# Attention in a two-layer decoder: row maximum from the high parts alone, full scores with keys on partitions, row sums on GpSimd

## The chip, the cores and the metric

One core of a Trainium2 chip. The time is the device time of one execution in microseconds (us). The core's engines are TensorE (PE in the profile; PEld its weight loads), VectorE (DVE), ScalarE (ACT), GpSimd (POOL) and SyncE (SP, which here only issues transfers). Each engine takes its own instructions in order and waits for the others by semaphores.

## What is computed

A Mamba-2 layer, then a latent-attention layer with 16 heads over 2048 tokens, in float32. The change touches only the attention, which per head h computes:

```python
s = (q_nope . k_nope + q_rope . k_rope) * 96 ** -0.5      # 64 + 32 features
p = softmax(where(key <= query, s, -inf))
o = p @ v                                                 # 64 features
```

A softmax row needs its maximum m, the exponentials exp(s - m), and their sum; o is divided by the sum at the end. Queries and keys are kept as a pair of parts, high and low, whose sum is the float32 number; three products (high by high, high by low, low by high) make one full score.

## The kernel before

`layers` runs the Mamba layer and the projections of the second layer, which write queries, keys, values and gates to DRAM. `attention` calls `heads`; `back` applies gate, reciprocal sums and the output projection. A scheduler sets the order of the instructions on DVE, ACT, POOL and SP; in `heads` the order on PE is as written.

A job is a head and a block of 512 queries (64 jobs). In a job the keys up to the diagonal are taken, 1 to 4 blocks of 512.

- `scores`: for each of the four groups of 128 queries, and each piece of up to 512 keys, three products (L86 to L88, in `mm3`) with **queries on the partitions**; Q is the weight, K moves. The last piece gets the causal mask as a product with the identity (L1014, L1016). DVE reduces each piece to its maximum (L1017); when all pieces of the group are there, to the negated row maximum nm (L1021). ACT then takes the exponential out of PSUM, with nm as its bias and the row sum as a second result (L1029), into the float32 tile Pr; DVE adds the sums of the pieces (L1033).
- `turn`: the value product needs keys on the partitions, so each 128 x 128 block of Pr is transposed on PE (L1044), four into a bank. `pair16` makes two float16 parts of it: ACT copies the high part (L117), DVE subtracts it from the PSUM bank for the low part (L118).
- `values`: two products with V as the weight (L1054, L1055), summed over the keys in one bank O. `finish` copies O to Os (ACT, L1061) and writes it out in two halves: SP stores the first (L1063), POOL issues an adding transfer of the second to the same place (L1067), which waits until the first has landed. After a head's last job the reciprocal sums are transposed (L1073) and stored.

The four groups' scores run 20 steps ahead (`LAG`); the table `CREDIT` says which transposes (T) and value products (V) follow each step. `load_k`, `load_v` and `load_q` fetch the next head's tiles on POOL's queue (L944 to L958). All PSUM tiles are banks of one pool, `pp`, with the tags mm and tr, four banks each. For `back` ACT and POOL split the output weights (L1127, L1128) during the last heads.

Of the kernel before, what the change touches and what calls it, by code (L numbers as in the profile page):

```python
# [21 lines left out]
P = 128  # L22
# [15 lines left out]
NP = 24  # L38
# [3 lines left out]
LAG = 20  # L42
DEPTH = 2
CREDIT = (
    (("VT",), ("TV",), ("VT",), ("TV",)),
    (("", "VTVT"), ("", "TTVV"), ("", "TTVV"), ("", "TTVV")),
    (("TT", "", "VVTV"), ("TV", "", "VTTV"), ("TV", "", "TTVV"), ("TTV", "", "TVV")),
    (("T", "", "", "VVTTVTV"), ("T", "V", "", "VTTVTV"), ("T", "V", "V", "TVTTV"), ("TV", "V", "", "TVTVT")),
)
MAGIC = 12582912.0  # L50
PSCALE = 32768.0
# [18 lines left out]
class Net:  # L70
# [180 lines left out]
    def constants(self, cp):  # L251
# [4 lines left out]
        self.mk = cp.tile([P, 2 * P], BF16, name="mk")  # L256
        at = 0
# [4 lines left out]
    def layer_constants(self, cp):  # L262
# [13 lines left out]
        nc.vector.memset(self.mk[:, P:], NEG)  # L276
        self.wdt = cp.tile([P, KD, 2, H], F16, name="wdt")
# [19 lines left out]
        nc.vector.tensor_copy(self.mk[:, 0:P], self.mask)  # L297

# [73 lines left out]
    def value_scale(self):  # L372
# [4 lines left out]
        for n in range(2):  # L377
# [18 lines left out]
            v.tensor_scalar(e, e, -25, None, ALU.add)  # L396
# [526 lines left out]
    def open_heads(self):  # L923
# [5 lines left out]
        self.load_k(0, 0, NB - 1)  # L929

    def load_vq(self):

        self.load_k(0, NB - 1, NB)
        self.load_q(0, 0)
        self.load_v(0)
        for n in range(1, NB):
            self.load_q(0, n)

    def load_k(self, h, lo, hi):

        nc, ts = self.nc, slice(lo * TB, hi * TB)
        if lo == 0:
            self.keys[h] = self.t(self.hp, "K", [96, 2, T], F32R, bufs=2)
        nc.gpsimd.dma_start(self.keys[h][0:64, :, ts], self.kn_d[h * 64:(h + 1) * 64, :, ts])  # L944
        nc.gpsimd.dma_start(self.keys[h][64:96, :, ts], self.kr_d[:, :, ts])

    def load_v(self, h):

        V = self.vals[h] = self.t(self.xq, "xT", [P, T // P, P], F16, bufs=8)
        self.nc.gpsimd.dma_start(V, self.v_d[:, h * P:(h + 1) * P].rearrange("(k p) d -> p k d", p=P))  # L950

    def load_q(self, h, n):

        nc, ts = self.nc, slice(n * TB, (n + 1) * TB)
        Q = self.quer[h, n] = self.t(self.xq, "xT", [96, 2, TB], F32R, bufs=8)
        nc.gpsimd.dma_start(Q[0:64], self.qn_d[h * 64:(h + 1) * 64, :, ts])
        nc.gpsimd.dma_start(Q[64:80], self.q1_d[h * 16:(h + 1) * 16, :, ts])
        nc.gpsimd.dma_start(Q[80:96], self.q2_d[h * 16:(h + 1) * 16, :, ts])  # L958

# [343 lines left out]
```

## Time and profile before

| | |
|---|---|
| median of 3 runs | 3202.09 us (3199.31 to 3207.09) |
| profiled execution | 3204.34 us, span 3202.6 us from first to last instruction |
| mean granted TensorE clock | 0.995 |
| busy share of the span | PE 96%, DVE 75%, ACT 60%, POOL 19% |
| first score product to last value product of the attention | 2087.6 to 3011.8 us |
| one head | 57.17 us |

The row of an instruction group reads: line, engine, operation, out<-in by the kernel's names, shape, count | busy us, mean ns of one | idle time of the engine just ahead of it, and what ended it. A row of one tile or line reads: least / median / most ns. A row of the timeline reads: start, duration, engine, line. Instructions of PE and ACT overlap their neighbours, so the distance between two starts is the price of one more, and the duration is its latency.

### The profile page before, as it was taken

How to read it: one execution, taken by the hardware profiler on the slowest of the kernel's cores; microseconds unless marked ns; L12 is line 12 of the kernel's file. 1: busy time of each engine (PE TensorE's matmuls, PEld its weight loads, DVE VectorE, ACT ScalarE, POOL GpSimd, SP SyncE). 2: the span in 40 equal slices, each digit the busy share in tenths (PEclk: the TensorE clock that was granted, in tenths of full speed). 3: DMA queues.
4: the chain of work that ended last, by engine and by line, in shares of the span. 5: the costliest groups of instructions: out<-in, count | busy, mean ns of one | idle time of the engine just before them, and what ended most of it. 6: DMA issues, size and time to landing. Idle time of an engine off the chain costs nothing.

```text
span 3202.6 us, 51345 instructions
## 1 busy us (share of the span) xinstructions
PE 3085.4 (96%) x17744; PEld 2163.4 (68%) x17744; DVE 2401.2 (75%) x5178; ACT 1914.1 (60%) x4817; POOL 609.1 (19%) x842
## 2 busy tenths in 40 slices
PE   6999999999999999999999999999999999999998
PEld 3455555666655566665878888877777777777777
DVE  7778887767677676767876665678888888888675
ACT  8667554444455444455645554477877778778522
POOL 0212122121122212212111211322212122222100
PEclk9999999999999999999999999999999999999999
DMA  8667645334443345334476656853444434443485
GB/s 285 229 214 230 229 144 194 127 126 145 141 157 130 115 151 189 127 128 142 141 271 218 225 190 194 265 111 78 95 81 84 81 78 96 79 97 99 101 270 159
DMA packets 207113, 497.61 MB, mean 155 GB/s; under 512 B 27746, under 2 KB 51042, under 8 KB 205412
## 3 DMA queue, kind: packets, MB, share of 16 engines
q1 hardware_dynamic: 165444, 370.04, 35.6%
q0 software_dynamic: 41408, 124.29, 15.9%
q8 instruction: 140, 2.29, 0.3%
q14 instruction: 121, 0.99, 0.1%
HBM read 362.22 MB, written 131.99 MB: 154 GB/s over the span
## 4 chain that ended last, share of the span: by engine, by line
PE 64%; DVE 13%; ACT 8%; DMA 8%; issue 6%; POOL 1%; SPq 0%; ACTq 0%; DVEq 0%; POOLq 0%
PE mm L86 13%; PE mm L87 12%; PE mm L88 12%; PE tr L1044 6%; PE tr L87 3%; PE tr L1054 3%; PE tr L1055 3%; PE tr L86 3%; PE tr L88 3%; DVE cacc L460 3%; DMA big<-cumT 2%; DMA wraw<-in_ssm_w_in_dram 1%; DVE big L634 1%; ACT Pr L1029 1%; PE tr L656 1%
## 5 line engine op out<-in xcount | busy, mean ns | idle before, releaser
L118 DVE SCALAR_TENSOR_TENSOR PTs<-tr,PTs 128x512 f16<-128x512 f32 (+3 forms) x640 | 374.9, 607 | 93.9 <-ACT PTs L117 86.8
L117 ACT ACTIVATE PTs<-tr 128x512 f16<-128x512 f32 (+3 forms) x640 | 328.5, 541 | 141.4 <-PE tr L1044 140.3
L1017 DVE TENSOR_REDUCE mx<-mm 128x1 f32<-128x512 f32 (+2 forms) x631 | 375.7, 608 | 45.7 <-PE mm L88 42.6
L1029 ACT ACTIVATE Pr<-mm,nm 128x512 f32<-128x512 f32 (+2 forms) x631 | 395.7, 636 | 23.1 <-DVE nm L1021 21.4
L1044 PE MATMUL tr<-pack,Pr 128*128 128x128 f32 x2176 | 317.6, 273 | 1.0 <-ACT Os L1061 0.9
L86 PE MATMUL mm<-K,xT 96*128 96x512 f32 (+2 forms) x639 | 288.2, 451 | 23.3 <-ACT Pr L1029 21.8
L86 PE MATMUL mm<-xT,wsp 128*128 128x512 f16 (+1 forms) x800 | 304.9, 381 | 0.3 <-DVE sz L484 0.3
L88 PE MATMUL mm<-xT,wsp 128*128 128x512 f16 (+1 forms) x800 | 303.4, 380 | 1.4 <-DVE wsp L118 1.3
L87 PE MATMUL mm<-xT,wsp 128*128 128x512 f16 (+1 forms) x800 | 303.7, 380 | 0.0
L1044 PEld LDWEIGHTS tr<-pack,Pr 128*128 128x128 f32 x2176 | 253.5, 141 | 49.7 <-ACT Os L1061 1.7
L648 ACT ACTIVATE Xw<-tr,d_wend 128x64 f32<-128x64 f32 x512 | 183.4, 359 | 133.3 <-DVE Xd L644 133.3
L460 DVE SCALAR_TENSOR_TENSOR cacc<-craw,pack,cacc 128x512 f32<-128x512 f32 x288 | 213.6, 764 | 30.5 <-ACT cacc L458 28.9
L86 PE MATMUL mm<-wsp,xT 128*128 128x512 f16 (+1 forms) x640 | 232.4, 363 | 1.6 <-ACT craw L454 1.6
L88 PE MATMUL mm<-K,xT 96*128 96x512 f32 (+2 forms) x639 | 231.6, 362 | 0.0
L87 PE MATMUL mm<-wsp,xT 128*128 128x512 f16 (+1 forms) x640 | 231.6, 362 | 0.0
L87 PE MATMUL mm<-K,xT 96*128 96x512 f32 (+2 forms) x639 | 231.4, 362 | 0.0
L88 PE MATMUL mm<-wsp,xT 128*128 128x512 f16 (+1 forms) x640 | 231.1, 362 | 0.0
L1054 PE MATMUL tr<-PTs,xT 128*128 128x512 f16 (+3 forms) x640 | 222.0, 348 | 0.1
L86 PE MATMUL mm<-wsp,yT 128*128 128x512 f32 x512 | 208.1, 409 | 13.3 <-DVE sz L484 4.7
L1055 PE MATMUL tr<-PTs,xT 128*128 128x512 f16 (+3 forms) x640 | 219.4, 347 | 0.0
L606 POOL TENSOR_TENSOR Xp<-Xw,Xp 128x512 fp32r<-128x512 f32 x64 | 81.8, 1278 | 711.3 <-ACT Xp L605 382.4
L88 PE MATMUL mm<-wsp,yT 128*128 128x512 f32 x512 | 203.0, 397 | 1.4 <-DVE yT L110 1.4
(411 smaller groups left out, 7418.2 us busy)
## 6 DMA issues: line engine op xcount, KB each, us to landing
wsp<-wi_d SPq DMA_DIRECT2D x96, 512.0 KB, 3.7
wsp<-wo_d SPq DMA_DIRECT2D x96, 512.0 KB, 3.5
big<-cumT SPq DMA_DIRECT2D x64, 512.0 KB, 4.9
wi_d<-wsp SPq DMA_DIRECT2D x32, 512.0 KB, 3.4
wo_d<-wsp SPq DMA_DIRECT2D x64, 256.0 KB, 2.5
xT<-qn_d POOLq DMA_DIRECT2D x64, 256.0 KB, 4.4
K<-kn_d POOLq DMA_DIRECT2D x15, 1024.0 KB, 9.2
hx<-in_ssm_w_in_dram SPq DMA_DIRECT2D x48, 256.0 KB, 4.3
```

Of the source, the lines that this page charges most:

```text
L86: mm(out, l_hi, r_hi, start=start, stop=False)
L87: mm(out, l_hi, r_lo, start=False, stop=False)
L88: mm(out, l_lo, r_hi, start=False, stop=stop)
L117: self.nc.scalar.activation(hi, src, AF.Copy, scale=scale)
L118: self.nc.vector.scalar_tensor_tensor(lo, src, scale, hi, ALU.mult, ALU.subtract)
L460: nc.vector.scalar_tensor_tensor(acc, raw[:, k:k + TB], wk[k], acc, ALU.mult, ALU.add)
L648: act(Xw[:, hc], px[:, hc], AF.Copy, scale=wend[:, h0 + h:h0 + h + 1])
L1017: v.tensor_reduce(mx[:, n:n + 1], s[:, :w], AX.X, ALU.max)
L1029: nc.scalar.activation(x[:, :w], s[:, :w], AF.Exp, bias=nm, accum_out=sm[:, n:n + 1])
L1044: nc.tensor.transpose(pt[:, j * P:(j + 1) * P], st["P"][j][kb], self.ident)
L1054: nc.tensor.matmul(st["O"][:, c], vals[h][:, kb, :], u[:, 0], start=kb == 0, stop=False)
L1055: nc.tensor.matmul(st["O"][:, c], vals[h][:, kb, :], u[:, 1], start=False, stop=kb == nk - 1)
```

## The change

**Maximum pass (`tops`).** For each group of 128 queries one product, high part by high part, goes over all keys, with the mask as before, into M: two banks, one buffer. DVE reduces both banks in one instruction (L1019, or L1021 for one bank): one step for up to two pieces. After a job's last step POOL negates the maximum, adds the constant `LIFT` (ln 64), splits the result into high and low parts (L1029 to L1031), and SP stores them to DRAM and reads them back as **row 96 of the query tile** (L1033, L1034). The key tile has a row 96 too: ones in the high part, zeros in the low, written to DRAM once when the kernel starts.

**Full scores (`probs`).** K is the weight, 128 keys; Q moves, 512 queries, 97 rows. So the three products give s - m with **keys on the partitions**, and nothing is transposed. A pair of key blocks fills S (two banks, two buffers). ACT takes the exponential twice, as float32 x and as float16 u, and DVE subtracts u from x for the low part (L1063). Of a block that the diagonal cuts, only the columns from there on are used.

**Row sums.** POOL adds each further x of the job onto the first one (L1068). Five pairs after the job's last value product, `total` sums over the partitions with four products of one column (128 x 128 weights, a column of twos).

**Order and queues.** The maximum pass runs `LEAD` = 22 units ahead (a head has 34 units, 4 qb + 2.5 for a job); then for each pair: maximum steps as far as the lead allows, full scores, and the value products of the pair before last. K, V and Q of the next heads are loaded on SP's queue, Q in or after `tops` of the job before. x has four buffers, the first x of a job four of its own. The attention has its own PSUM pool (M 2, S 4, O 2 banks), `back` another. The scaling by 32768 and its reverse move into the constants.

Core of the diff (a line of ... where lines are left out):

```diff
-    def load_k(self, h, lo, hi):
+    def load_k(self, h, lo, hi, queue):
...
-            self.keys[h] = self.t(self.hp, "K", [96, 2, T], F32R, bufs=2)
+            self.keys[h] = self.t(self.hp, "K", [97, 2, T], F32R, bufs=2)
...
+        def tops(h, qb):
...
+                for m in range(max(n // 2, 1)):
+                    s = self.t(ap, "M", [P, 2, TB], bufs=1)
+                    for i in range(both):
+                        c0, last = (2 * m + i) * w, 2 * m + i == n - 1
+                        mm(s[:, i, :w], Q[0:96, 0, qs], K[0:96, 0, c0:c0 + w], start=True, stop=not last)
...
+                    if both == 2:
+                        v.tensor_reduce(mx[:, m, j:j + 1], s[:, :, :w], AX.XY, ALU.max)
...
+                        gp.tensor_scalar(nm, mx[:, 0], -1.0, LIFT, ALU.mult, ALU.add)
+                        gp.tensor_copy(hl[:, 0], nm)
+                        gp.tensor_tensor(hl[:, 1], nm, hl[:, 0].bitcast(F32), ALU.subtract)
+                        d = self.nm_d[h, qb]
+                        nc.sync.dma_start(d.rearrange("a j p -> p a j"), hl.bitcast(F32))
+                        nc.sync.dma_start(Q[96:97].bitcast(F32), d.rearrange("a j p -> (a j p)").rearrange("(o a t) -> o a t", o=1, a=2))
...
+        def probs(h, qb, m, st):
...
+            s = self.t(ap, "S", [P, 2, TB], bufs=2)
+            x = self.t(sp, "x" if m else "x0", [P, 2, TB], bufs=4)
...
+                self.mm3(s[:, i, w0:], K[:, 0, ks], K[:, 1, ks], Q[:, 0, w0:], Q[:, 1, w0:], True, jj < 0)
...
+            for i, c in parts:
+                act(x[:, i, c], s[:, i, c], AF.Exp)
+                act(u[:, 0, i, c], s[:, i, c], AF.Exp)
+                v.tensor_tensor(u[:, 1, i, c], x[:, i, c], u[:, 0, i, c], ALU.subtract)
+            if m == 0:
+                st["sum"] = x[:, 0]
+            for i in range(0 if m else 1, 2):
+                c = cols[i]
+                gp.tensor_tensor(st["sum"][:, c], st["sum"][:, c], x[:, i, c], ALU.add)
...
-        def turn(h, qb, kb, st):
-
-            jj = max(kb - 4 * qb, 0)
-            pt = self.t(self.pp, "tr", [P, TB], bufs=4)
-            for j in range(jj, 4):
-                nc.tensor.transpose(pt[:, j * P:(j + 1) * P], st["P"][j][kb], self.ident)
...
+        def total(h, qb, acc):
+
+            ps = self.t(ap, "M", [P, 2, TB], bufs=1)
+            for j in range(4):
+                mm(ps[:, 0, j:j + 1], acc[:, j * P:(j + 1) * P], self.two, start=True, stop=True)
...
+            for m in range(2 * qb + 2):
+                while there < at + LEAD:
+                    step = next(lead, None)
...
+                u, cols = probs(h, qb, m, st)
+                at += size[qb] / (2 * qb + 2)
+                held.append((h, qb, m, st, u, cols))
+                settle()
```

How the order of instructions moves is seen on two engines. POOL before, in one of the first heads: its queue from two jobs' adding transfers to the loads for the next head (xT is a query tile, K the keys).

```order
L1067 DMA o_d<-Os_22583 64x512
L1067 DMA o_d<-Os_22721 64x512
L956 DMA xT_22940<-qn_d 64x2x512
L957 DMA xT_22940<-q_d 16x2x512
L958 DMA xT_22940<-q_d 16x2x512
L944 DMA K_23109<-kn_d 64x4096
L945 DMA K_23109<-kr_d 32x4096
```

POOL after the change, the last block of queries of the first head (x is the tile that the sums gather in and the tiles added to it, nm and hl the negated maximum and its parts, o_d the adding transfer):

```order
L1068 TENSOR_TENSOR x_4080_21922<-x_4080_21922 128x512
L1068 TENSOR_TENSOR x_4080_21922<-x_4080_21922,x_21948 128x512 x2
L1068 TENSOR_TENSOR x_4080_21922<-x_4080_21922,x_21975 128x512 x2
L1090 DMA o_d<-Os_21965 64x512
L1068 TENSOR_TENSOR x_4080_21922<-x_4080_21922,x_21998 128x512 x2
L1068 TENSOR_TENSOR x_4080_21922<-x_4080_21922,x_22025 128x512 x2
L1068 TENSOR_TENSOR x_4080_21922<-x_4080_21922,x_22048 128x512 x2
L1029 TENSOR_SCALAR nm_22081<-mx_21938 128x4
L1030 CAST hl_22082<-nm_22081 128x4
L1068 TENSOR_TENSOR x_4080_21922<-x_4080_21922,x_22089 128x512
L1031 TENSOR_TENSOR hl_22082<-nm_22081,hl_22082 128x4
```

The loads are gone from POOL's queue; in their place stands a row of additions, and the adding transfer of the job before and the small instructions for a later job's maximum stand between them.

DVE before, at the diagonal of a job (mm and tr are PSUM banks, PTs is in SBUF):

```order
L1021 TENSOR_REDUCE nm_25678<-mx_25628 128x1
L118 SCALAR_TENSOR_TENSOR PTs_25664<-tr_25659,PTs_25664 128x512
L118 SCALAR_TENSOR_TENSOR PTs_25671<-tr_25667,PTs_25671 128x384
L1017 TENSOR_REDUCE mx_25681<-mm_25684 128x1
L118 SCALAR_TENSOR_TENSOR PTs_25692<-tr_25689,PTs_25692 128x256
L118 SCALAR_TENSOR_TENSOR PTs_25697<-tr_25695,PTs_25697 128x128
L1017 TENSOR_REDUCE mx_25681<-mm_25716 128x1
```

DVE after the change, at the start of a job (M is in PSUM, x and PTs in SBUF):

```order
L1019 TENSOR_REDUCE mx_22535<-M_22540 128x1
L1063 TENSOR_TENSOR PTs_22520<-x_4197_22519,PTs_22520 128x1024
L1019 TENSOR_REDUCE mx_22535<-M_22566 128x1
L1063 TENSOR_TENSOR PTs_22546<-x_22545,PTs_22546 128x1024
L1019 TENSOR_REDUCE mx_22535<-M_22590 128x1
L1063 TENSOR_TENSOR PTs_22573<-x_22572,PTs_22573 128x1024
```

A reduction of a maximum step and a subtraction for a pair take turns; the subtraction has lost its operand in PSUM and reads two tiles in SBUF.

More of the change, by code (lines that the diff above doesn't have):

```diff
@@ L1087, in heads @@
-        units = [(h, qb, kb, states[n]) for n, (h, qb) in enumerate(jobs) for kb in range(4 * qb + 4)]
-        held = []
-        def work(what):
-            if what == "T" and units:
-                a = units.pop(0)
-                held.append((a, turn(*a)))
-            elif what == "V" and held and (len(held) > DEPTH or not units):
-                a, (u, c) = held.pop(0)
-                values(*a, u, c)
-        step = 0
-        for credit in ahead():
-            step += 1
-            if step > LAG:
-                for what in credit:
-                    work(what)
@@ L1110, in back @@
+        while held or late:
+            settle(True)
     def back(self):
```

266 lines of the change are left out of this document (141 added, 125 removed).

## The prediction

> **What bounds the kernel now.** I read the busy shares first, then one head of the attention in the table by stretches, then the chain of work that ended last, the groups by form, and the waits. All of the change lies in the attention, so its stretch sets the price. Over the whole span PE is the busiest engine:
>
> ```profile
> PE 3085.4 (96%) x17744; PEld 2163.4 (68%) x17744; DVE 2401.2 (75%) x5178; ACT 1914.1 (60%) x4817; POOL 609.1 (19%) x842
> ```
>
> One head repeats exactly. In the chain the same pair of PTs instructions returns after 57.16 us, and between them stand pieces of eight back-to-back transposes:
>
> ```profile
> 2341.33 1.29 DVE PTs L118 x2
> ...
> 2353.82 0.87 PE tr L1044 x8
> ...
> 2398.49 1.29 DVE PTs L118 x2
> ```
>
> A stretch of one period (time; then PE, PEld, DVE, ACT, POOL busy with counts):
>
> ```profile
> 2388.88:2446.05 57.17, 55.90 (x356) 42.88 (x354) 48.05 (x115) 45.25 (x125) 12.04 (x19) 1.00 0.42 84
> ```
>
> PE is bound here, at the full granted clock (1.00); POOL works 12 us of 57. A busy PE is not PE at its peak, so I take its price from distances between starts:
>
> ```profile
> 2350.61 0.39 PE L87 MATMUL mm<-K,xT 96*128 96x512 f32 x1
> ...
> 2350.84 0.40 PE L88 MATMUL mm<-K,xT 96*128 96x512 f32 x1
> ```
> ```profile
> 2341.74 0.38 PE L1054 MATMUL tr<-PTs,xT 128*128 128x512 f16 x1
> ...
> 2341.96 0.38 PE L1055 MATMUL tr<-PTs,xT 128*128 128x512 f16 x1
> ```
>
> So 512 columns cost 0.23 us in f32r, 0.22 in f16, and one transpose 0.87 / 8 = 0.11. By the loops, a head of before has 17,536 score columns three times over (103 x 0.23 = 23.6), 136 transposes (15.0), 34,816 value columns (68 x 0.22 = 15.0) and 16 mask products (about 1): 54.6 of 57.2 us.
>
> **The change, per head of attention.** *PE.* The transposes go (-15.0). The full scores stay, turned round: 53,760 columns, 24.2. The maximum pass adds one product over 17,536 columns (7.9) and 16 more masks (1). The row sums become 16 products of one column; the nearest row,
>
> ```profile
> L144 PE MATMUL tr<-ss,ones 128*128 128x1 f32 x2 | 0.6, 363 | 5.5 <-DVE ss L183 5.5
> ```
>
> and the transpose bound them by 0.11 and 0.36; I take 0.2, nearer the transposes that also stand in a row, so 3.2. PE then has 24.2 + 1 + 7.9 + 1 + 15.0 + 3.2 = 52.3. The gain is 2.3 us a head, not 15.
>
> *ACT* has two exponentials of 1024 columns for each pair of key blocks in place of one exponential with its sum and one copy for each block:
>
> ```profile
> L117 ACT ACTIVATE PTs<-tr 128x512 f16<-128x512 f32 x448 | 258.6, 600 | 90.0 <-PE tr L1044 88.8
> ...
> L117 ACT ACTIVATE PTs<-tr 128x256 f16<-128x256 f32 x64 | 25.6, 400 | 34.3 <-PE tr L1044 34.3
> ```
>
> By this slope 1024 columns take 1.0 us: 12 full pairs x 2.0 + 4 diagonal sets x 3.4 + 2.4 for Os = 40, under today's 45. *DVE* reduces both banks of a maximum step at once:
>
> ```profile
> L1017 DVE TENSOR_REDUCE mx<-mm 128x1 f32<-128x512 f32 x395 | 269.1, 685 | 44.9 <-PE mm L88 42.6 <-PE mm L1016 0.3
> ...
> L1017 DVE TENSOR_REDUCE mx<-mm 128x1 f32<-128x256 f32 x126 | 52.3, 415 | 0.3 <-PE mm L1016 0.3
> ```
>
> That is 1.05 ns a column and 0.145 fixed: 24 steps, 17,536 columns, 21.9 us. The low parts no longer come from PSUM: they are x - u, both in SBUF. Nearest rows for 1024 and 512 columns with two SBUF inputs:
>
> ```profile
> L636 DVE TENSOR_TENSOR big<-big,CB x64: 1209/1224/1227, 95.4 to 1557.2; 128x1024 f32<-128x1024 f32 x64
> ```
> ```profile
> L110 DVE TENSOR_TENSOR wsp<-wraw,wsp x68: 670/686/695, 1591.7 to 2058.1; 128x512 fp32r<-128x512 f32 x68
> ```
>
> 12 x 1.22 + 4 x (0.69 + 0.55 + 0.69) = 22.4; with the small ones DVE has 46, against 48 today.
>
> *POOL* is where the work goes. Each key block after the first of a job is added to the row sums: 24 additions of 512 columns a head, and four each of 384, 256 and 128. The rows that price them, and the small ones for the negated maximum:
>
> ```profile
> L606 POOL TENSOR_TENSOR Xp<-Xw,Xp x64: 1267/1275/1312, 101.8 to 1560.6; 128x512 fp32r<-128x512 f32 x64
> L606 POOL TENSOR_TENSOR Ct<-BC,Ct x60: 447/488/1047, 62.4 to 1533.1; 128x128 fp32r<-128x128 f32 x60
> ```
> ```profile
> L453 POOL COPY craw<-halo 128x3 f32<-128x3 f32 x96 | 63.3, 661 | 155.0 <-DVE cacc L460 146.1 <-ACT Xw L648 3.8 <-DVE ss L185 3.2
> L1067 POOL DMA_DIRECT2D o_d<-Os x64 | 54.8, 856 | 455.6 <-ACT PTs L117 215.4 <-DMA o_d<-Os 149.3 <-ACT Pr L1029 86.7
> ...
> L455 POOL COPY halo<-craw 128x3 f32<-128x3 f32 x96 | 33.5, 349 | 180.3 <-ACT craw L454 180.0
> ```
>
> 24 x 1.275 + 4 x (1.00 + 0.72 + 0.45) = 39.3 (the middle two by the line between the ends). Twelve small instructions at 0.35, between 0.18 and 0.66: 4.2. Four o_d issues at 0.856: 3.4. Each addition reads what the one ahead of it wrote; a dependent pair on DVE starts 0.20 apart at 0.16 long, so 36 x 0.04 = 1.4:
>
> ```profile
> 10.19 0.16 DVE L226 TENSOR_TENSOR rss<-rsy 128x4 f32<-128x4 f32 x1
> 10.39 0.16 DVE L228 SCALAR_TENSOR_TENSOR rsq<-rsx,rss 128x4 f32<-128x4 f32 x1
> ```
>
> POOL alone: 48.3 us a head, which would still fit under PE. But it does not work alone. First a DVE instruction's own time (least, median, most), then a place where the two engines meet:
>
> ```profile
> L460 DVE SCALAR_TENSOR_TENSOR cacc<-craw,pack,cacc x288: 733/745/1772, 50.6 to 1479.0; 128x512 f32<-128x512 f32 x144
> ```
> ```profile
> 1474.53 1.40 DVE L460 SCALAR_TENSOR_TENSOR cacc<-craw,pack,cacc 128x512 f32<-128x512 f32 x2
> 1475.86 1.75 DVE L678 SCALAR_TENSOR_TENSOR y<-y,down,sz 128x512 f32<-128x512 f32 x1
> ```
> ```profile
> 1475.35 1.71 POOL L606 TENSOR_TENSOR Sp<-st,Sp 128x512 fp32r<-128x512 f32 x1 [4.49 <-ACT Sp L605]
> ```
>
> A POOL subtraction of 1.275 took 1.71: it ended at 1477.06, 1.13 after the pair of L460, which have two SBUF inputs, had ended at 1475.93. The next DVE instruction, of the same kind and size as L460's 0.745, took 1.75 and ended at 1477.61, 0.55 after POOL. The two exclude each other. In the attention of today POOL's two-input instructions run beside DVE at 84% busy without a stretch; there DVE's big operand comes from PSUM:
>
> ```profile
> L1128 POOL TENSOR_TENSOR W<-wr,W x4: 2347/2362/2394, 2892.7 to 2921.7; 128x1024 fp32r<-128x1024 f32 x4
> ```
>
> The change makes 24 DVE subtractions a head of the excluding kind. By that row one of 512 columns holds the port 0.55 us, one of 1024 then 1.1; of this the next addition's start (1.275 less the 1.13 that POOL needed once free, and the 0.04) runs beside it. Each pushes POOL's row of additions back by 0.92, or 0.37 and 0.24 at 512 and 384 columns: 12 x 0.92 + 4 x (0.37 + 0.24 + 0.37) = 15.0. POOL needs 48.3 + 15.0 = 63.3 us a head. Bounds: small ones at 0.18, and 7.6 / 48 of the subtractions falling where POOL issues or does small ones, give 59; small ones at 0.66 give 67.
>
> The Trainium skill has this as a rule that speaks against the change: SBUF — State Buffer, "Who interferes with whom", says that a DVE instruction with two SBUF inputs and a GpSimd one that reads SBUF take a shared port in turn, the whole instruction long, while DVE with one SBUF input doesn't contend. The trace agrees (1.75 for 0.745, 1.71 for 1.275). Whole durations laid end to end would give 39.3 + 22.4 + 7.6 = 69.3 us a head, about 3420; the sum above goes by the measured overlap.
>
> POOL would so replace PE as the bound: ACT's next x must wait until POOL has added the x of four pairs before, and PE waits for ACT. (63.3 - 57.2) x 16 = +98 us.
>
> *Waits and moves.* Q, K and V loads leave POOL for SP, some 15 issues a head at about 0.45. SP now also stores and rereads the maximum; it stands behind POOL's small instructions, and Q, K, V and o_d behind it. A landing takes
>
> ```profile
> o_d<-Os SPq DMA_DIRECT2D x64, 128.0 KB, 3.6
> ```
>
> so 4 x 7 us a head wait in SP, hidden by a lead of 22 of the 34 units of a head (37 us of 57). Row-sum products wait in PE's order for POOL's last addition, all of PE behind them; five pairs of delay cover POOL's lag of four. Maximum products share one buffer, so PE waits for DVE's reduction: in the steady part a pair of PE work (over 2 us) lies between.
>
> At the start nothing covers it: the lead is 18 steps in turn, each a product, a reduction and two signals; by the rows above 0.9 to 2.1 us each, 26 in all. Today the first transpose comes 14.7 us after the first score:
>
> ```profile
> 2087.58 0.28 PE L86 MATMUL tr<-K,xT 96*128 96x256 f32 x1
> ```
> ```profile
> L1044 PE MATMUL tr<-pack,Pr x2176: 270/273/329, 2102.3 to 3010.6; 128*128 128x128 f32 x198
> ```
>
> +11. POOL's eight W and K splits (2.36 each), now in its idle time, come among the last heads' additions: six ahead of the end, +14. At the kernel's start a store of zeros stands in SP behind a DVE memset at about 10.3 us, inside
>
> ```profile
> 3.61 7.05 SPq L175 DMA_DIRECT2D big<-in_ssm_w_in_dram  x8
> ```
>
> which may hold four of these loads 0 to 4 us: +2. Without a maximum pass in the last 0.65 head, -3.
>
> **Sum.** The profiled execution took 3204.3 (span 3202.6 and 1.7 around it); 98 + 11 + 14 + 2 - 3 = +122, so 3326, and 3324 against the median, 2 us lower.
>
> **Rivals.** *The port doesn't decide (faster).* If subtractions mostly fall where POOL is idle, POOL stays near 50 and PE remains the bound at 52.3 and today's 2.6 us of stalls: -2.3 x 16 + 13 = 3180; with no stalls at all 3138; with 2 us more, 3212. It decides once POOL and its pushes stay under 55 us, so at less than half the price of a push. For it: 48.3 alone fits, and one addition chain has gaps. Against: the rows above show full exclusion, and POOL would hold the port 34 of 55 us (39.3 less 36 starts of 0.14). *POOL's order costs more (slower still).* The o_d issue on POOL waits for SP's store, with additions now behind it, where today it was idle:
>
> ```profile
> 2346.46 0.86 POOL L1067 DMA_DIRECT2D o_d<-Os  x1 [4.27 <-DMA o_d<-Os]
> ```
>
> Four such a head, less the pushes that fall into them (some 5), give 63.3 + 12, or 3520; two of them some 3420. For it: SP's stores stand behind POOL's own small instructions. Against: in POOL's order several additions lie between, by which time the store has landed if POOL lags.
>
> **How the numbers follow.** POOL bound by the port: 0.72, with its own range 3257 (59 us a head) to 3385 (67). POOL's waits on top: 0.08, 3420 to 3520. PE still the bound: 0.20, of which 0.12 below 3192 and 0.08 within 0.3% (9.6 us, about what a measurement of this kernel can tell from no change). So faster 0.12, same 0.08, slower 0.80. The range reaches from 3190, where the faster outcomes begin, to 3430, which takes in two waits a head; it leaves out 0.12 and some 0.04.
>
> **What would show it.** Right: a head of about 63 us; POOL above 85% busy there; its 512-column additions (L1068) at a mean of 1.5 to 1.9 where 1.275 is their own time; DVE's L1063 of 1024 columns well above 1.22; ACT waiting for POOL's x; PE idle a sixth of the time. Wrong: a head under 57 with both near their own times, or PE's idle time put down to M, O or the Q row in place of x.

## The result, and the profile after

The changed kernel takes 3653.51 us (median of 4 runs, 3648.9 to 3656.22), the kernel before 3204.58 beside it: a ratio of 1.1402, 95% interval 1.138 to 1.1424. The sign was as forecast; the size, +449 us, is nearly four times the forecast +122 and outside the range.

The page of the changed kernel: busy shares, then the rows of POOL and of the granted clock in forty slices, then DMA packets.

```profile
PE 3277.6 (90%) x17040; PEld 2197.6 (60%) x17040; DVE 2465.0 (68%) x4222; ACT 1781.0 (49%) x3665; POOL 1306.6 (36%) x1379
...
POOL 0212122212221221211211246656666767666600
PEclk9999999999999999999999978888888888877899
...
DMA packets 302351, 498.25 MB, mean 137 GB/s; under 512 B 125092, under 2 KB 148420, under 8 KB 300649
```

The same two rows on the page of before:

```profile
PEclk9999999999999999999999999999999999999999
...
DMA packets 207113, 497.61 MB, mean 155 GB/s; under 512 B 27746, under 2 KB 51042, under 8 KB 205412
```

No engine has become the bound: in the attention POOL stands at 6 and 7 tenths. Two things are new. The clock row, all 9 before, is 7 and 8 over the attention. And packets under 512 bytes are 125,092, where before had 27,746.

One head in the table by stretches, from one head's end to the next (time; then PE, PEld, DVE, ACT, POOL busy with counts; then the granted clock):

```profile
2615.48:2696.58 81.10, 68.90 (x309) 45.10 (x309) 50.75 (x54) 37.03 (x54) 56.49 (x52) 0.83 0.45 59
```

A head takes 81 us where it took 57.17. POOL is busy 56.5 of them, PE stands idle 12.2, and its clock is 0.83. The groups show what PE and its neighbours waited for:

```profile
L1061 ACT ACTIVATE x<-S 128x1024 f32<-128x1024 f32 (+2 forms) x384 | 306.2, 797 | 689.7 <-PE S L82 274.6
...
L1013 PE MATMUL M<-K,xT 96*128 96x320 f32 (+8 forms) x704 | 283.6, 481 | 178.4 <-DVE mx L1019 84.2
L80 PE MATMUL S<-xT,K 97*128 97x512 f32 (+2 forms) x640 | 299.1, 467 | 73.7 <-DMA xT<-nm_d 73.6
```

ACT's largest named wait is for PE's scores. Those for POOL's x come close behind (259.1 us in 94 waits, in the view of line 1068), so this sign of the prediction came true, but with a POOL that isn't full and waits itself (below). PE waits ahead of the maximum products (L1013) for DVE's reduction and ahead of the scores (L80) for the query row that comes back from nm_d: the M and the Q row that the prediction named as what would show it wrong.

**The query row.** SP's timeline of the changed kernel (start, duration; L1033 stores the maximum, L1034 reads it back, L1086 is the o_d store):

```profile
2603.89 0.38 SPq L1033 DMA_DIRECT2D nm_d<-hl  x1
2604.37 0.54 SPq L948 DMA_DIRECT2D K<-kn_d  x1
2615.75 0.23 SPq L1034 DMA_DIRECT2D xT<-nm_d  x1
2616.03 0.46 SPq L1086 DMA_DIRECT2D o_d<-Os  x1
```

Then POOL and PE at the same place:

```profile
2622.23 0.84 POOL L1090 DMA_DIRECT2D o_d<-Os  x1 [10.12 <-DMA o_d<-Os]
2622.85 7.51 POOL L1068 TENSOR_TENSOR x<-x,x 128x512 f32<-128x512 f32 x6
```
```profile
2620.62 0.79 PE L80 MATMUL S<-xT,K 97*128 97x512 f32 x1 [4.08 <-DMA xT<-nm_d]
```

The store of the maximum is 1,024 pieces of four bytes. SP issues it at 2603.89 and can issue the read that depends on it at 2615.75, 11.9 us later. The o_d store stands behind, at 2616.03, so POOL, which waits for its landing, stands 10.1 us at its adding transfer, with six additions behind it. In the table of waits, between 2200 and 3300 us (us in total, times, longest), first SP, then POOL:

```profile
SPq L1034 <- DMA nm_d<-hl: 447.1, 52, 11.1
SPq L1033 <- POOL hl L1031: 342.2, 40, 14.8
```
```profile
POOL o_d L1090 <- DMA o_d<-Os: 295.6, 37, 11.5
```

It is a ring: SP waits for POOL's hl, then 8.6 us each time for the landing; POOL waits for the o_d store behind it, 8.0 us each; its next hl comes late for that. SP's standing is only part of it. One job later SP issues the o_d store right behind that of the maximum, without waiting, and POOL can go on only 10.4 us after that issue (SP, then POOL):

```profile
2637.64 0.38 SPq L1033 DMA_DIRECT2D nm_d<-hl  x1
2638.12 0.54 SPq L1086 DMA_DIRECT2D o_d<-Os  x1
```
```profile
2648.48 0.85 POOL L1090 DMA_DIRECT2D o_d<-Os  x1 [8.30 <-DMA o_d<-Os]
```

Thirteen of POOL's waits are of this kind, 9.3 to 13.3 us after the issue. So the store in four-byte pieces holds up the transfer that is issued behind it, too.

**The clock.** PE's timeline of the changed kernel, some lines left out, at one place:

```profile
2587.22 0.95 PE L1097 MATMUL M<-two,x 128*128 128x1 f32 x8
2588.44 0.62 PE L1013 MATMUL M<-K,xT 96*128 96x384 f32 x2 [0.28 <-DVE ri L1100]
2590.11 1.01 PE L1013 MATMUL M<-K,xT 96*128 96x384 f32 x2 [1.05 <-DVE mx L1019]
...
2591.58 0.63 PE L81 MATMUL S<-xT,K 97*128 97x512 f32 x1
2592.01 0.63 PE L82 MATMUL S<-xT,K 97*128 97x512 f32 x1
...
2598.91 0.40 PE L81 MATMUL S<-xT,K 97*128 97x512 f32 x1
2599.14 0.40 PE L82 MATMUL S<-xT,K 97*128 97x512 f32 x1
```

PE waits 0.28 and 1.05 us for DVE at the one maximum buffer. The clock's record is at half from 2589.74 to 2596.56. Right after the waits, products of 512 columns start 0.43 apart; at 2598.9 they are back at 0.23. DVE in the same stretch:

```profile
2585.90 2.07 DVE L1063 TENSOR_TENSOR PTs<-x,PTs 128x1024 f16<-128x1024 f32 x1
2588.20 0.18 DVE L1100 RECIPROCAL ri<-M 128x4 f32<-128x4 f32 x1 [0.23 <-PE M L1097]
2589.10 0.96 DVE L1019 TENSOR_REDUCE mx<-M 128x1 f32<-128x768 f32 x1 [0.71 <-PE M L1013]
```

PE waits for DVE, and DVE for PE, in turn. In PE's order the row-sum products (2587.22) and two maximum steps (2588.44, 2590.11) stand directly behind one another here, all of them into M; with one buffer nothing else can happen at such a place.

The trace holds the clock's changes, and it is either full or half. So a head divides into three parts: idle (no product runs), clock (half of the time in which products run at half clock) and work (the rest: what PE would need at full clock). Means over some ten heads, between the copies to rT that end each head; before is the stretch of 57.17 that the prediction shows:

| kernel | time | head | idle | clock | work |
|---|---|---|---|---|---|
| before | 3204.6 | 57.2 | 1.3 | 0 | 55.9 |
| after | 3653.5 | 81.3 | 14.1 | 10.1 | 57.1 |
| e1_rows | 3530.2 | 75.1 | 9.5 | 8.6 | 57.0 |
| e2_half | 3574.1 | 76.2 | 10.1 | 9.1 | 57.0 |
| e3_rows_half | 3538.1 | 75.5 | 9.8 | 8.8 | 56.9 |
| e4_psum | 3625.2 | 81.1 | 14.7 | 8.7 | 57.7 |
| e6_two | 3471.5 | 71.7 | 8.1 | 6.2 | 57.4 |
| e7_two_alone | 3677.5 | 84.7 | 18.7 | 8.0 | 58.0 |
| e8_rows_late_two | 3462.8 | 70.7 | 8.2 | 4.9 | 57.7 |
| e9_no_total | 3463.3 | 70.6 | 12.0 | 5.6 | 53.1 |
| e10_few_reductions | 3340.7 | 62.2 | 3.0 | 2.3 | 56.9 |
| e11_extra_product | 3485.5 | 72.7 | 5.3 | 2.0 | 65.5 |
| e12_three | 3516.4 | 75.1 | 15.3 | 3.2 | 56.6 |
| e13_psum | 3316.3 | 62.4 | 3.9 | 0.5 | 58.0 |
| e14_late | 3644.6 | 81.0 | 14.1 | 9.9 | 57.1 |
| e15_psum_few | 3290.9 | 60.8 | 2.2 | 1.4 | 57.2 |

Of the 24.1 us that a head grew, 12.8 are idle time, 10.1 the clock, and 1.2 more work. By PE's table of waits (2290 to 3100 us, ten heads) the idle 14.1 of the changed kernel are 9.5 ahead of products into M and 4.6 for the query row. Each experiment is one run beside the kernel before on the same chip (3203 to 3209), so a few us between two of them say nothing.

### The profile page after: what moved, and what is told of

The parts are those of the page before. It is cut to its first block, busy times and chain, and to the rows that moved or that the text cites. A ratio compares the mean times of both kernels' runs of the same rounds, so it can differ in the third digit from the quotient of the medians.

```text
span 3649.0 us, 48838 instructions
## 1 busy us (share of the span) xinstructions
PE 3277.6 (90%) x17040; PEld 2197.6 (60%) x17040; DVE 2465.0 (68%) x4222; ACT 1781.0 (49%) x3665; POOL 1306.6 (36%) x1379
## 2 busy tenths in 40 slices
DMA packets 302351, 498.25 MB, mean 137 GB/s; under 512 B 125092, under 2 KB 148420, under 8 KB 300649
## 5 line engine op out<-in xcount | busy, mean ns | idle before, releaser
L1068 POOL TENSOR_TENSOR x<-x,x 128x512 f32<-128x512 f32 (+3 forms) x512 | 677.5, 1323 | 35.6 <-ACT x L1061 4.4
L1061 ACT ACTIVATE x<-S 128x1024 f32<-128x1024 f32 (+2 forms) x384 | 306.2, 797 | 689.7 <-PE S L82 274.6
L1063 DVE TENSOR_TENSOR PTs<-x,PTs 128x1024 f16<-128x1024 f32 (+2 forms) x384 | 483.4, 1265 | 123.3 <-ACT PTs L1062 120.9
L1019 DVE TENSOR_REDUCE mx<-M 128x1 f32<-128x640 f32 (+7 forms) x320 | 317.9, 993 | 329.6 <-PE M L1017 242.1
L1013 PE MATMUL M<-K,xT 96*128 96x320 f32 (+8 forms) x704 | 283.6, 481 | 178.4 <-DVE mx L1019 84.2
L80 PE MATMUL S<-xT,K 97*128 97x512 f32 (+2 forms) x640 | 299.1, 467 | 73.7 <-DMA xT<-nm_d 73.6
L1062 ACT ACTIVATE PTs<-S 128x1024 f16<-128x1024 f32 (+2 forms) x384 | 305.5, 796 | 0.0
L80 PE MATMUL mm<-xT,wsp 128*128 128x512 f16 (+1 forms) x800 | 304.8, 381 | 0.0
L1013 PEld LDWEIGHTS M<-K,xT 96*128 96x128 f32 x704 | 142.3, 223 | 241.8 <-DVE mx L1019 103.9
L81 PE MATMUL S<-xT,K 97*128 97x512 f32 (+2 forms) x640 | 262.8, 411 | 0.0
L82 PE MATMUL S<-xT,K 97*128 97x512 f32 (+2 forms) x640 | 262.0, 409 | 0.0
L80 PE MATMUL mm<-wsp,xT 128*128 128x512 f16 (+1 forms) x640 | 232.5, 363 | 3.3 <-ACT craw L457 3.3
L1080 PE MATMUL O<-PTs,V 128*128 128x512 f16 (+1 forms) x600 | 234.1, 396 | 0.0
L1081 PE MATMUL O<-PTs,V 128*128 128x512 f16 (+1 forms) x600 | 227.1, 389 | 3.4 <-DVE PTs L1063 3.2
L80 PE MATMUL mm<-wsp,yT 128*128 128x512 f32 x512 | 206.9, 406 | 11.4 <-DVE hs L522 4.2
```

Source lines behind the costliest of these rows:

```text
L80: mm(out, l_hi, r_hi, start=start, stop=False)
L81: mm(out, l_hi, r_lo, start=False, stop=False)
L82: mm(out, l_lo, r_hi, start=False, stop=stop)
L1013: mm(s[:, i, :w], Q[0:96, 0, qs], K[0:96, 0, c0:c0 + w], start=True, stop=not last)
L1019: v.tensor_reduce(mx[:, m, j:j + 1], s[:, :, :w], AX.XY, ALU.max)
L1061: act(x[:, i, c], s[:, i, c], AF.Exp)
```

## The experiments

The first four set three theories against each other: A, SP's landing and POOL's wait behind it; B, the port that the prediction rests on; C, PE at its lower clock.

**e1_rows.** The maximum is stored in pieces of 32 bytes (a partition's eight numbers side by side), and the read puts them in order.

```
-nc.sync.dma_start(d.rearrange("a j p -> p a j"), hl.bitcast(F32))
-nc.sync.dma_start(Q[96:97].bitcast(F32), d.rearrange("a j p -> (a j p)").rearrange("(o a t) -> o a t", o=1, a=2))
+nc.sync.dma_start(d.rearrange("a j p -> (a j p)").rearrange("(p a j) -> p a j", a=2, j=4), hl.bitcast(F32))
+flat = d.rearrange("a j p -> (a j p)")
+nc.sync.dma_start(Q[96:97].bitcast(F32).rearrange("o a (j p) -> o (a j) p", p=P), flat.rearrange("(o p aj) -> o aj p", o=1, aj=8))
```

> Edit: the negated maximum is stored with 32 bytes in a piece (128 pieces) in place of 4 bytes (1024 pieces); the read back then gathers 1024 pieces of 4 bytes, but no instruction on SP waits for the read. Theory A (the store lands 10.3 us after its issue, SP stands at the read behind it, the stores of o_d stand behind that, and POOL at its adding transfer): SP's wait falls to about 3.5 us, POOL's waits at o_d from 302 us to under 100, a head from 81 to 64-68 us, time 3380 to 3440. Theory B (the exclusion of DVE's and POOL's two-input instructions is the main loss): POOL fills the gain with waits for the port, under 100 us gained, above 3550. Theory C (TensorE at a granted clock of 0.83 is the bound): the clock and the time stay, above 3550.

Measured 3530.20. In its tables of waits, SP and POOL:

```profile
SPq L1035 <- DMA nm_d<-hl: 48.2, 32, 3.9
```
```profile
POOL o_d L1091 <- DMA o_d<-Os: 22.3, 16, 4.9
```

SP's wait for the landing falls from 447.1 us (52 times, 8.6 each) to 48.2 (32 times, 1.5 each), and POOL's wait from 295.6 to 22.3 us in all, by an edit that doesn't touch POOL; the order of the instructions is the same on every engine. Where SP issues the o_d store right behind that of the maximum, POOL now goes on 2.8 to 5.2 us after the issue. The number of small packets isn't the cause: the read still fetches four-byte pieces, and packets under 512 bytes are 133,732, more than in the changed kernel. The mechanism of A holds and is worth 123 us. It was expected to be worth more: a head still takes 75, and the time lies between A's range and that of B and C.

**e2_half.** The second half of the outputs goes to a scratch tensor from SP, so POOL has no adding transfer; the low half of the values is left out.

```
-gp.dma_start(od, o[64:128, :], accum_op=ALU.add)
+nc.sync.dma_start(self.scrap, o[64:128, :])
```

> Edit: the second half of each o tile is stored to a scratch place from SP in place of POOL's adding transfer, so POOL never waits for o_d. This leaves the low half of the values out of the result. Theory A: POOL loses 19 us of waits and 3.4 us of issues in each head; SP's waits at the maximum's store stay, and with them PE's waits for the query row (9 us a head): a head of 64 to 70 us, time 3380 to 3470. Theory B and C: above 3550.

Measured 3574.11. POOL is freed from the wait, and a head is 76.2. That is a gain of 79 us, but outside A's range, in that of B and C.

**e3_rows_half.** Both edits.

> Edit: both of the above (the low half of the values is left out of the result). Theory A: neither engine waits for SP any more; POOL's own work and the port are left, 60 to 64 us a head by the sum of the prediction less 3.4 us of issues: 3270 to 3350. Theory B: above 3500. Theory C: above 3500, PE at 0.8 to 0.85 of its clock.

Measured 3538.12, no better than e1_rows alone, and in the range of B and C. With the rows landing soon, POOL's wait is gone already; something else holds a head at 75. Its table of waits for PE, 2290 to 3100 us, shows where:

```profile
PE M L1013 <- DVE mx L1019: 35.2, 33, 1.4
PE M L1013 <- DVE mx L1021: 30.7, 22, 2.3
PE M L1104 <- DVE ri L1101: 12.3, 11, 1.1
PE M L1013 <- DVE ri L1101: 9.1, 33, 0.3
```

All of it stands ahead of a product into M.

**e4_psum.** DVE makes the low part as scores (PSUM) times zero times u; so it comes out zero, and the operation has one input in SBUF.

```
-v.tensor_tensor(u[:, 1, i, c], x[:, i, c], u[:, 0, i, c], ALU.subtract)
+v.scalar_tensor_tensor(u[:, 1, i, c], s[:, i, c], 0.0, u[:, 0, i, c], ALU.mult, ALU.mult)
```

> Edit: DVE's low part of the exponentials reads S in PSUM and u in SBUF (zero times S times u) in place of x and u, so it has one SBUF input; count and sizes stay, and the low part is zero, which leaves it out of the result. POOL's additions then meet no other instruction at the port: their mean falls from 1.48 to 1.28 us for 512 columns. Theory A: POOL's busy time falls from 55 to about 47 us a head, its waits for o_d stay: 3520 to 3600. Theory B: 3300 to 3400. Theory C: no change.

Measured 3625.22, a head of 81.1. A stretch of its attention:

```profile
2600.00:2681.00 81.00, 65.63 (x304) 43.20 (x302) 42.38 (x54) 35.65 (x52) 45.26 (x54) 0.85 0.50 61
```

POOL falls to 45 us, DVE to 42, and the kernel gains 28: while SP's ring sets the pace, the port costs little.

That left C in a sharper form, theory D: PE and DVE wait for each other at the one maximum buffer, and PE's clock falls because it stands. The experiments from here on test it.

**e6_two.** e3_rows_half with two maximum buffers of one bank in place of one of two banks (44 reductions a head in place of 24).

```
-s = self.t(ap, "M", [P, 2, TB], bufs=1)
+s = self.t(ap, "M", [P, TB], bufs=2)
```

> With the rows stored in 32-byte pieces and half of the outputs left out, as in e3_rows_half, and the maximum products in two buffers of one bank instead of one buffer of two. Theory D (what is left is the ring PE, DVE, PE through the one maximum buffer: in e3_rows_half PE stood idle 10 us a head, nearly all of it ahead of a product into M, and the granted clock then fell to half for stretches that cost another 8.9 us a head): most of both goes, a head takes 57 to 61 us instead of 75.4, the granted clock in the attention is above 0.95, the time is 3230 to 3330. Rival E (the in-order rows of ACT, DVE and POOL wait for one another and set the pace, PE's waits only show it): the wait moves to the score or output buffers, a head stays above 71 us and the clock below 0.91, the time is 3470 to 3540. Theory B (port): POOL's 52.5 us a head show as a bound, a head of 62 to 66, 3330 to 3400.

Measured 3471.49: a gain of 67 where over 200 was expected. Time and head (71.7) lie in rival E's range, but the waits have not moved as E has it: PE still waits at M, 69.6 us for the reductions alone (2290 to 3100 us). A second buffer helps, but isn't enough.

**e7_two_alone.** The same edit on the changed kernel.

> Only the maximum buffers are changed, into two of one bank; rows and outputs as in the changed kernel. Theory D with A: of the idle time of PE ahead of M and of the query row (143 us in 800) the M part of 88 goes, the row part stays, and the clock still falls after waits for the row: a head of 69 to 75 us instead of 81.3, 3450 to 3560. Rival E: 3610 to 3660.

Measured 3677.47, 24 us slower than the changed kernel and above both ranges. SP's waits there:

```profile
SPq L1032 <- DMA nm_d<-hl: 444.6, 51, 11.0
```

The row's landing still rules, so the buffer gains nothing; why it loses a little was not tried. A limit that stands behind another can't be priced alone.

**e8_rows_late_two.** Rows, two buffers, and POOL's adding transfer written later in the code, in the step that contracts the row sums; everything is computed.

> Everything is computed: rows stored in 32-byte pieces, two maximum buffers of one bank, and POOL's adding transfer issued five pairs later, when the store that it waits for has long landed. Theory D with A: POOL has 55 us a head of work of its own, PE 52 to 57, so a head of 58 to 63 us and 3240 to 3350. Rival E: 3470 to 3540. Theory B: POOL busy above 90% in the attention, and the time at the upper end of the first range or beyond it, up to 3400.

Measured 3462.83, far above D's range and 7 us below E's. The same kernel was timed again:

> e8_rows_late_two again, timed in rounds: all its theories have it at 3455 to 3475, a ratio to the kernel before of 1.078 to 1.085. It is the fastest that computes everything, and would still be slower than before.

Measured 3455.38 (3450.52 to 3467.57, 4 runs), a ratio of 1.08 to the kernel before, interval 1.0776 to 1.0825. It is the fastest of the kernels that compute everything and still 8% slower than before. One head of it (2625.91 to 2697.23), and its waits for PE:

```profile
2625.91:2697.23 71.32, 62.88 (x310) 42.04 (x309) 55.59 (x78) 37.13 (x53) 54.88 (x53) 0.93 0.39 68
```
```profile
PE M L1011 <- DVE mx L1016: 79.5, 97, 2.3
```

Of PE's waits at M, 94.7 us with those for the row sums, 89.5 stand where the product ahead of it in PE's order goes into M as well. POOL is busy 54.9 of 71.3 us.

**e14_late** was to tell what moving the adding transfer did by itself.

```
-                gp.dma_start(od, o[64:128, :], accum_op=ALU.add)
-                late.append([LATE, h, qb, st["sum"]])
+                late.append([LATE, h, qb, st["sum"], od, o])
...
-        def total(h, qb, acc):
+        def total(h, qb, acc, od, o):
+            gp.dma_start(od, o[64:128, :], accum_op=ALU.add)
```

> The changed kernel with one edit: POOL's adding transfer is issued five pairs later, so that the store it waits for has landed. Everything is computed; the row's landing in SP and the one maximum buffer stay. Theory A (POOL's wait for the store stands ahead of its additions): as e2_half, which left the transfer out, 3550 to 3610. Rival G (e2_half gained by the missing traffic, or the row's wait takes the whole place): 3630 to 3660.

Measured 3644.56. The edit did nothing: the order of the instructions is the same in both kernels on every engine, since a scheduler sets it and not the place in the code. POOL still waits:

```profile
POOL o_d L1094 <- DMA o_d<-Os: 291.5, 36, 11.3
```

The time lies where rival G put it, but says nothing for G. In e8_rows_late_two the move does nothing either: its order is that of e7_two_alone on every engine, so these two differ by the way the rows are stored and read alone, and that is worth 215 us with two buffers, where it was 123 with one. That POOL's wait is SP's row is shown by e1_rows.

**e9_no_total.** e3_rows_half, with the row sums neither contracted nor turned: scaling is left out.

> As e3_rows_half, and the row sums are neither contracted by PE nor turned: their reciprocals are left out and a copy of some columns of the sums stands in their place, so outputs are not scaled rightly. One maximum buffer as before. Theory D: PE loses 4.1 us a head of products (four times 1.02) and 3.7 us a head of waits that the row sums have in the one buffer, and with them one or two of the four falls of the clock: a head of 63 to 68 us instead of 75.4, 3340 to 3430. Rival E: above 3500.

Measured 3463.26, between the two ranges. Work falls by 3.8 us a head, as the sixteen row-sum products should, but idle time rises by 2.2: part of what PE no longer does it waits instead. The waits that the row sums had at M are gone, but those for the reductions rise, from 66 us in e3_rows_half (35.2 + 30.7) to 138.

**e10_few_reductions.** From e8_rows_late_two; only the last maximum step of each row block is reduced. The maximum is partial, and the exponentials are of a twentieth of the score.

```
-v.tensor_reduce(mx[:, m, j:j + 1], s[:, :w], AX.X, ALU.max)
+if last:
+    v.tensor_reduce(mx[:, 0, j:j + 1], s[:, :w], AX.X, ALU.max)
```

> From e8_rows_late_two; DVE reduces only the last maximum step of each row block (16 of 44 a head), so that the other steps free their buffer at once; the maximum is then partial, and the exponentials are taken of a twentieth of the score. PE's products are all there. Theory D (what is left in e8, 8.2 us a head of idle time and 4.9 of half clock beside 57.7 of work, comes from PE waiting for DVE at the maximum buffers): idle 2 to 4, clock loss 0 to 2, a head of 60 to 63 us instead of 70.7, 3285 to 3345. Rival E (ACT's and POOL's rows, with POOL 55 us busy): the wait moves to the scores, a head stays above 67 us, above 3400.

Measured 3340.70, a head of 62.2, inside D's range: 122 us come back when DVE frees the maximum buffers at once, though PE's products are all there. Rival E is out. The edit also takes 28 reductions a head from DVE's row, so that its subtractions come sooner too; how much is the buffers' alone isn't told apart.

**e11_extra_product.** From e8_rows_late_two; PE makes the first product of each score block twice.

```
+mm(s[:, i, w0:], K[:, 0, ks], Q[:, 0, w0:], start=True, stop=True)
 self.mm3(s[:, i, w0:], K[:, 0, ks], K[:, 1, ks], Q[:, 0, w0:], Q[:, 1, w0:], True, jj < 0)
```

> From e8_rows_late_two; the first product of each score block is made twice, 40 more products and 8 us more work for PE a head, with nothing else changed. Theory D (PE comes to the maximum buffers too early, stands there, and loses its clock by standing): the added work fills the idle time and holds the clock up: work 66, idle 2 to 4, clock loss 0 to 2, a head of 68 to 72 us where it was 70.7, so 3420 to 3490. Rival F (PE's own work sets the pace, the clock falls for a reason of its own): all of it is added, a head of 78 to 80 us, 3580 to 3620.

Measured 3485.50, in D's range. PE does 7.8 us more a head, and a head grows by 2.0: idle time falls by 2.9 and the clock's part by 2.9. One of the heads in the table by stretches, at full clock throughout (others still lose some):

```profile
2635.24:2706.54 71.30, 65.58 (x350) 46.33 (x349) 55.23 (x78) 37.23 (x53) 55.13 (x53) 1.00 0.37 68
```

Rival F is out: the clock doesn't fall of itself. PE loses it by standing.

**e12_three.** From e8_rows_late_two; three maximum buffers and one output buffer.

> From e8_rows_late_two; three maximum buffers, and one output buffer instead of two. Everything is computed. Theory D: PE's waits at the maximum fall by half or more, those for the output's copy come in at up to 1.5 us four times a head: a head of 64 to 69 us, 3350 to 3430. Rival E: 70 to 73 us, 3450 to 3500.

Measured 3516.43. The waits at M fall from 79.5 to 24.2 us, but a wait for the query row came in:

```profile
PE S L80 <- DMA xT<-nm_d: 128.6, 13, 12.2
...
PE M L1011 <- DVE mx L1016: 24.2, 26, 1.4
```

The time, above both ranges, decides neither way. Where the row's wait comes from was not tried further.

**e13_psum.** e4's edit on e8_rows_late_two; the low part is zero.

> From e8_rows_late_two; the low part is made from the scores in PSUM and comes out zero, so DVE's operation no longer has two inputs in SBUF, and is shorter, DVE some 7 us a head. Theory D with B: DVE is sooner at the reductions, POOL and DVE don't hold each other up: idle 4 to 6, clock loss 2 to 4, a head of 64 to 68 us instead of 70.7, 3355 to 3420. Port of no weight any more: 3440 to 3470.

Measured 3316.28, better than the theories had it: 147 us, five times what the same edit gave on the changed kernel. POOL's additions over some thirteen heads, and a head in the table by stretches:

```profile
L1067 POOL TENSOR_TENSOR x<-x,x 128x512 f32<-128x512 f32 (+3 forms) x417 | 453.6, 1088 | 102.0 <-ACT x L1060 80.3
L1067 POOL TENSOR_TENSOR x<-x 128x512 f32<-128x512 f32 (+1 forms) x52 | 63.1, 1214 | 95.8 <-ACT x L1060 95.8
```
```profile
2626.18:2688.08 61.90, 58.08 (x310) 39.32 (x309) 45.69 (x78) 37.15 (x54) 44.91 (x53) 1.00 0.45 79
```

Both engines are at their own times, POOL now waits for ACT, and PE holds its clock. DVE's low part here, and in e8_rows_late_two over eleven heads:

```profile
L1062 DVE SCALAR_TENSOR_TENSOR PTs<-S,PTs 128x1024 f16<-128x1024 f32 (+2 forms) x313 | 290.4, 931 | 48.1 <-ACT PTs L1061 42.2
```
```profile
L1062 DVE TENSOR_TENSOR PTs<-x,PTs 128x1024 f16<-128x1024 f32 (+2 forms) x265 | 348.3, 1321 | 27.9 <-ACT PTs L1061 26.2
```

The edit takes the port away, and the operation itself is no shorter for it: 0.93 us on the mean is what the prediction's rows gave for two inputs in SBUF without POOL beside them (22.4 us for 24 subtractions). So the 9 us a head by which these operations are shorter in all are the port's. The scheduler's order differs in places from that of e8_rows_late_two; what that adds isn't told apart.

**e15_psum_few.** e10 and e13 in one.

> e10_few_reductions and e13_psum in one: partial maximum, low part zero, so DVE is neither late at the maximum buffers nor shares a port with POOL. If ring (D) and port (B) are all that is left above PE's own work of 57 to 58 us a head, idle falls to 1 to 2.5 and the clock loss to under 0.5: a head of 58.5 to 61 us, 3255 to 3300. If a third limit holds (rival E: the rows of ACT and POOL, or the wait for the query row), nothing is added to what each gave: a head of 62 us or more, above 3310.

Measured 3290.87, a head of 60.8 with 57.2 of work. Ring and port together bring a head to within 3.6 us of PE's own work, so no third limit of size is left. What then stands between this and the kernel before, 88 us, is 16 x 3.6 = 58 and some 30 that don't come from the steady heads.

## Why the prediction was wrong, step by step

- **"4 x 7 us a head wait in SP, hidden by a lead of 22 of the 34 units"** is the first step that failed. The sum was not far off, though the landing was priced by o_d's 3.6 us, a store of whole rows: SP stood 8.6 us at each store of four-byte pieces, 33 us a head against 28. What failed is "hidden": the o_d store behind it lands late, POOL, which makes the next row, waits for that landing itself, and PE then waits for the query row (4.6 us a head). e1_rows: 123 us. The Trainium skill, DMA: Bandwidth & Descriptors, Specifications, gives 512 bytes as the least transfer for the full rate, and says that smaller ones are read, modified and written. No run here tests that limit: pieces of four and of 32 bytes both lie below it, and SP's wait was 8.6 us with the one and 1.5 with the other.
- **"Maximum products share one buffer ... a pair of PE work (over 2 us) lies between"** is the second. PE's order is not so. The lead lets two or three maximum steps stand in a row, and the row sums use the same buffer, so that 10 of the 29 uses of M in a head stand directly behind another one. There PE can only wait for DVE: of its 94.9 us of waits at M (2290 to 3100 us) 87.2 are at such places, and 7.7 behind score or value products. In DVE's order a subtraction of 1.22, lengthened to 1.6 by the port, may stand ahead of the reduction and make the wait longer. e10_few_reductions: 122 us. An order of PE that spreads the steps over the pairs was not tried.
- **The clock, left at 1.00.** The prediction took every PE price at the full clock of before. In the changed kernel PE stood 14.1 us a head and lost 10.1 more at half clock; e11_extra_product shows cause and effect. A wait of PE was priced once and cost 1.7 times its length.
- **POOL as the bound at 63.3 us** failed, with its chance of 0.72. Its work was well priced: the 417 + 52 additions of e13_psum, 36 to a head, take 453.6 + 63.1 us, 39.7 a head against 39.3. In the changed kernel, over the twelve heads from 2209.62 to 3189.25,

```profile
L1068 POOL TENSOR_TENSOR x<-x,x 128x512 f32<-128x512 f32 (+3 forms) x384 | 505.4, 1316 | 23.6
L1068 POOL TENSOR_TENSOR x<-x 128x512 f32<-128x512 f32 (+1 forms) x48 | 70.0, 1459 | 4.4 <-DVE PTs L1063 4.4
```

  they take (505.4 + 70.0) / 12 = 48.0, 8.3 more. The small instructions for the maximum take 4.9 a head where e13_psum has 2.3, so the pushes are some 11 us a head where 15.0 were forecast. At 56.5 of 81 us POOL isn't full. It nearly is in e10_few_reductions, where little is left of PE's waits at M:

```profile
2290.00:3100.00 810.00, 757.76 (x3922) 519.35 (x3922) 539.66 (x560) 477.94 (x685) 734.10 (x660) 0.95 0.44 78
```

  There POOL is busy 91% of the time, and a head of 62.2 is near the forecast 63.3. So the bound that was forecast stood close behind the waits that came first; with the port away as well (e15_psum_few) a head takes only 1.4 us less.
- **The port** is real: 512-column additions in the changed kernel take 1.49 on the mean and DVE's 1024-column subtractions 1.60, where 1.28 and 1.22 were their own in the prediction's rows. What failed is the way to the time. In the changed kernel it does not cost by filling POOL, but by making DVE late, for which PE waits at the maximum buffers: the edit that takes it away gains 28 us while SP's ring rules, 147 once that is gone.
- **PE at 52.3** was too low: its work is 57.1 at full clock, above the 55.9 of before. The row sums were nearly right (3.8 by e9_no_total, 3.2 forecast). By the distances between starts in e13_psum the maximum products take 13.5 us a head, not 7.9: 0.31 each for some 400 columns. Why they are dearer than their columns isn't shown. So the gain of 2.3 us a head was not there either, and with 57 us of work against a head of 57.2 before, nothing was to be won even without a wait.
- **The rival "POOL's order costs more"**, at 0.08, had the right place (37 waits of 8.0 us in some thirteen heads) and a time of 3420 to 3520, still too low: it was added to a bound of POOL's that didn't act here, without PE's idle time and clock.
- **The ends.** From the first maximum product to the first score 33 us pass, where 26 were put. The splits of W, priced at 14 us in all, come in heads of 100 and 102 us where 81 is usual, about 40 us; but in e1_rows the same two heads take 78 and 87 where 75 is usual, so 14 was the price without the ring. The last head is 18 shorter than the usual one, but that of before was 12.5 shorter already: the change saves 5.6 there, not 3.

## What to carry to other kernels

Busy times that fit under the bound don't make a kernel fit: before, scores and transposed blocks had four buffers each between PE and DVE, now the maximum has one, and the two wait for each other at lower busy shares (DVE 51 of 81 us, where it was 48 of 57). Read in PE's order how many uses of one buffer stand directly behind one another. Where a change puts a result through memory, price its landing by a store of the same piece size, and follow what stands behind it in that queue to the engine that makes the next one. And where PE is to wait at all, add the clock: in these runs it cost between 0.1 (e13_psum) and 0.9 (e1_rows) of the idle time on top.

## What the hardware showed

**The clock follows idle time in windows of 3.41 us.** The records change only in steps of 3.41 us, on one grid. In the sixteen kernels of the table, 2200 to 3100 us, windows at full clock with under 0.6 us of idle PE were followed by half clock 4 times in 2574, with 0.6 to 1.2 us 90 in 432, with 1.2 to 1.9 us 210 in 292, above 1.9 us 141 in 141. Full clock came back 443 times, each after a window with less than 0.05 us of idle time. Idle time is not all that counts: in the kernel before, 13 windows with 1.2 to 1.5 us all stayed at full clock; what else decides isn't known. The Trainium skill, TensorE: Matmul & The Clock Gate, "HAM oscillation — how this bites in real kernels", asks for no idle gaps above some 3.4 us. By that rule none of the changed kernel's waits at M, 2.8 us at most, would have cost the clock; the trace differs, since 0.96 us in two pieces were enough in the window that ends at 2589.74 (the waits ahead of 2588.44 and 2590.11 above).

**Four-byte pieces in a store** held SP's queue 8.6 us for 4 KB, 32-byte pieces 1.5 (means of the waits at the read), and the next store with it: it landed 9.3 to 13.3 us after its issue, and 2.8 to 5.2 behind 32-byte pieces.

**The port touches the smallest operations.** In e8_rows_late_two, over eleven heads, DVE's maximum over 8 columns with both inputs in SBUF takes 1.22 us. At 2326.14 and 2353.27 it ends 0.02 us after the addition that POOL has beside it. In e13_psum, where that addition ends sooner after its start, it takes 0.24 (first e8_rows_late_two, then e13_psum):

```profile
L1022 DVE TENSOR_TENSOR mx<-mx 128x8 f32<-128x8 f32 x22 | 26.9, 1222 | 0.0
```
```profile
L1022 DVE TENSOR_TENSOR mx<-mx 128x8 f32<-128x8 f32 x26 | 6.3, 243 | 0.0
```
